# The recurrence of an RWKV-7 layer: another order of work on VectorE and ScalarE, keys scaled earlier, final norms on other banks

## The chip, the cores and the metric

The kernel runs on one core of a Trainium2 chip. The metric is the device time of one execution in microseconds, as the median of several runs. The engines are PE (matrix products; PEld is its loading of weights), DVE (VectorE), ACT (ScalarE), POOL (GpSimd) and SP (SyncE, which issues all the DMAs named here).

## The reference, cut to what matters

A trunk of two layers on 1024 prompt rows with 16 meta rows ahead of them, and on 64 sample rows (8 sequences of 8), 1104 columns in all. Layer 0 is a gated DeltaNet and isn't touched. Layer 1 is RWKV-7 time mixing with 16 heads of 64:

```python
kk = l2norm((k * k_k).reshape(B, T, H, N))
k = k * (1.0 + (a - 1.0) * k_a)
decay = jnp.exp(-jnp.exp(w))
...
def step(S, inp):
    r_t, k_t, v_t, d_t, kk_t, b_t = inp
    S = (S * d_t[:, :, None, :]
         + jnp.einsum('bhvk,bhk->bhv', S, -kk_t)[..., None] * b_t[:, :, None, :]
         + v_t[..., None] * k_t[:, :, None, :])
    return S, jnp.einsum('bhvk,bhk->bhv', S, r_t)
...
y = (y - mean) * lax.rsqrt(var + GN_EPS) * lnx_w.reshape(H, N) + lnx_b.reshape(H, N)
y = y + jnp.sum(r_h * k_h * r_k, -1, keepdims=True) * v_h
y = y.reshape(B, T, D) * jax.nn.silu(z)
return y @ w_o, S, xn[:, -1]
```

After the layer come a residual add and one final RMSNorm (`finish` in the kernel).

## The kernel before

Layer 1 computes the recurrence in chunks of 64 rows. The 1104 columns are three segments (384, 384, 336), the 16 heads eight pairs, so there are 24 **items** n = 8 s + p, each with six chunks. Within a chunk the decays are cumulated: `cs` is their running sum, Dp = exp(-c cs) scales what reads the state, iD = exp(c cs) what writes it. A chunk's inner triangular system is inverted beforehand.

**Projections** (`projections`): PE runs the dense tiles of r, v and z; beside them `system_steps` makes for each item the scaled keys kk (stored as `kpd`), the reads al (`ald`), the plain keys k2 (`k2d`) and the triangular system, `system_inverse` inverts it on GpSimd, `system_merge` finishes it (`ttd`). VectorE also makes the low halves of the weights here.

**The wave** (`wave`): 52 steps tau. In step tau up to three items are in work, item n with its chunk ci = tau - 2n. A step has the phases 0, 1, 1.5, 2 and 3, and the order of all instructions is that in which Python emits them, engine by engine; nothing is reordered. `step_solve` multiplies state and reads (matmuls into `xX` and `rA`, then ACT scales X, L115); `step_inner` applies the inverse (matmuls, then ACT writes UV); `step_values` starts the next step's values; `step_state` adds UV into the state's bank `rA` and into the output, in the same bank, DVE writes the state S (L1921), then ACT copies y (L1922). `step_old` (`pre` on ACT) follows after phase 2.

Around this, `rwkv_item` puts the work of an item into (step, phase, priority), with T = 2n its first step; within a phase the lower priority goes first. Ahead of T: `load` (DMAs, T-4), `exps` (Dp and iD on ACT, T-3), `reads` and `writes` (products on DVE into AR and BK, T-3), `pair` (product of r, r_k and k2, DVE, T-3), `halves` (its split for PE, ACT and POOL, T-2), `scores` (24 matmuls `fG`, then masks on DVE, T-2 and T-1), `values` (transposes of v, ACT copies them into UV, T-2), `bonus` (two matmuls, then `rbv` on DVE, T-2), `keys` (transposes of BK, T-1). Behind it: `stats` for each chunk (DVE), then `rwkv_finish` in five parts: the variance and the power on POOL (L160); the end of the reciprocal root on DVE and the normalised y on POOL (L1945; for n above 21 on ACT with a bias `gnb`); transposes of y and `t` (L1953); `lz` (L1955); the split into yh (ACT) and yl (POOL).

`fill` works off two further lists in shares of a step: the output products `project_out` (three matmuls for each of 4 item tiles, weights by `Stream.take`, which casts a tile with whi on ACT and wlo on POOL and fetches another, then an addition L2042 on DVE), and `finish` for the first two segments: four transposes `dfin` into a bank, a square on ACT (its sum is wanted), a product with the weight on DVE (L2078), twice; then a root, and a scaling on POOL (L2093) and the output DMA.

PSUM has eight banks: tag "r" 3, "f" 2, "x", "z" and "d" 1 each. A tag's next user waits until the last reader of the bank is done.

Of the kernel before, what the change touches and what calls it, by code (L numbers as in the profile page):

```python
# [88 lines left out]
class Builder:  # L89
# [1477 lines left out]
    def system_steps(self, Q, B):  # L1567
# [30 lines left out]
        nc.vector.tensor_tensor(a, a, k, op=ALU.mult)  # L1598
        nc.sync.dma_start(self.ald[Q.n], al)
# [93 lines left out]
    def rwkv_item(self, n, put):  # L1693
# [13 lines left out]
        def load(*names):  # L1707
            src = dict(cs=(self.csd[p], 1), r=(self.rd[p], 2), v=(self.vd[p], 2))
            for x in names:
                if x == "al":  # L1710
                    P.AR = t(self.fp, [128, 6, 2, 64], "AR", 5)
                    nc.sync.dma_start(P.AR[:, :, 0, :], c6(self.ald[n]))
                elif x == "kp":
                    P.BK = t(self.fp, [128, 6, 2, 64], "BK", 2)
                    nc.sync.dma_start(P.BK[:, :, 1 - P.x, :], c6(self.kpd[n]))
                elif x == "tt":
                    P.TT = self.TTz[n % len(self.TTz)]
                    for h in (0, 1):
                        q = slice(64 * h, 64 * h + 64)
                        nc.sync.dma_start(P.TT[q, h].rearrange("p c k -> p (c k)"), self.ttd[n][q])  # L1720
                elif x == "k2":
                    ld[x] = t(self.fp, [128, 384], "fldk2", 2)
                    nc.sync.dma_start(ld[x], self.k2d[n])
                else:
                    d, b = src[x]
                    ld[x] = t(self.fp, [128, 384], "fld" + x, b)
                    nc.sync.dma_start(ld[x], d[:, c0:c0 + 384])

        def exps():
            P.Dp, P.iD = t(self.fp, [128, 384], "fDp", 1), t(self.fp, [128, 384], "fiD", 1)  # L1730
            self.act(P.Dp, ld["cs"], AF.Exp, scale=-self.DEC)
            self.act(P.iD, ld["cs"], AF.Exp, scale=self.DEC)
# [8 lines left out]
        def writes():  # L1741
            nc.vector.tensor_tensor(P.BK[:, :, P.x, :], c6(ld["k2"]), c6(P.iD), op=ALU.mult)

        def pair():
            P.pr = t(self.fp, [128, 384], "pr", 1)
            nc.vector.scalar_tensor_tensor(P.pr, ld["r"], pc("rwkv_r_k"), ld["k2"], op0=ALU.mult, op1=ALU.mult)
# [55 lines left out]
        put(T - 3, 1, exps, 2)  # L1802
        put(T - 3, 2, reads, 2)
        put(T - 3, 3, writes, 1.5)
        put(T - 1 - (n < 3), 2 + (n < 3), lambda: load("tt"), 0)
        put(T - 3, 3, pair, 6)
        put(T - 2, 1, halves, 1)
        put(T - 2, 1, lambda: scores(0), 2)
        put(T - 2, 2, values, 3)
        put(T - 2, 3, bonus, 3)  # L1810
# [3 lines left out]
        if s == 0:  # L1814
# [3 lines left out]
            put(T - 2, 2, go, 5)  # L1818
# [15 lines left out]
        for ci in range(6):  # L1834
            put(T + ci + 1, 1 if ci < 5 else 0, lambda ci=ci: stats(ci), 2.5 if ci < 5 else 0)
        if n < 22:
            f = self.rwkv_finish(P, 0, 6)
            at = [(T + 6, 0, 2), (T + 6, 2, 1.8), (T + 8, 0, 3), (T + 8, 1, 2.2), (T + 8, 2, 0)]
            plans = [(f, at + [(T + 8, 3, 5)] * (s == 2))]
        elif n == 22:  # L1840
            plans = [(self.rwkv_finish(P, 0, 6), [(T + 6, 0, 2), (T + 6, 1, 2), (T + 7, 0, 2.9), (T + 7, 0, 2.95), (T + 7, 1, 2.3),
                                                     (T + 7, 3, 5)])]
        else:
            plans = [(self.rwkv_finish(P, 0, 4), [(T + 4, 1, 3), (T + 4, 3, 2), (T + 5, 0, 3), (T + 5, 0, 3.1), (T + 5, 1, 2)]),
# [63 lines left out]
    def step_state(self, P, ci):  # L1908
# [7 lines left out]
        for h in (0, 1):  # L1916
            self.mmx(P.pY[hs[1 - h]], G[:, ci, h, 64:128], UV[:, ci, h, :], self.first(P, hs[1 - h]))
        if c == 1:
# [3 lines left out]
        nc.scalar.copy(P.y[:, ci], P.pY)  # L1922

    def rwkv_finish(self, P, a, b):
# [6 lines left out]
        zg = t(ap, [128, 384], "lz", 2)  # L1931
# [37 lines left out]
    def rwkv_sample_read(self, P):  # L1969
# [9 lines left out]
        sp = self.ps("f", 2, "sn")  # L1979
# [80 lines left out]
    def finish(self, s, x2):  # L2060
# [3 lines left out]
        for q in range(3):  # L2064
            tt = 3 * s + q
            nr = 80 if tt == 8 else 128
            tags = [(R, R), (R, ("x", 1)), (("d", 1), R)][q] if s == 2 else [("d", 1)] * 2
# [464 lines left out]
    def wave(self, zin, stay, last, pool):  # L2532
# [4 lines left out]
        Z, DD = ("z", 1), ("d", 1)  # L2537
# [16 lines left out]
        jobs += [(lambda s=s, a=a: out(s, a, a + 4, Z, DD), 16, 15 + 16 * s + 2 * a, 23 + 16 * s + 2 * a) for s in (0, 1) for a in (0, 4)]  # L2554
        jobs += [(lambda: out(2, 0, 4, Z, ZF), 16, 47, 51), (lambda: out(2, 4, 6, Z, ZF), 8, 51, 52)]

        more = [(lambda: self.finish(0, X2[0]), 12, 31, 38), (lambda: self.finish(1, X2[1]), 12, 47, 51.5)]
# [102 lines left out]
```

## Time and profile before

| | us |
|---|---|
| median of 3 runs | 2259.64 |
| lowest, highest | 2253.32, 2263.17 |
| profiled execution, its own time | 2267.2 |
| its span (first to last instruction) | 2265.5 |
| start of the first X of the wave in the span | 1791.77 |
| granted clock of TensorE, mean over the span | 0.966 |

Over the span PE is busy for 93%, DVE for 63%, ACT and POOL for 56% each. A line such as "L1921 DVE ... | 31.6, 278 | 14.5 <-PE rA L133 9.6" says: line of the kernel, engine, operation, tiles and shapes, count; busy us in all and mean ns of one; idle us of the engine ahead of them, and what ended it. Matmuls are pipelined, so that a PE that counts as busy need not be at its peak.

### The profile page before, as it was taken

How to read it: one execution, taken by the hardware profiler on the slowest of the kernel's cores; microseconds unless marked ns; L12 is line 12 of the kernel's file. 1: busy time of each engine (PE TensorE's matmuls, PEld its weight loads, DVE VectorE, ACT ScalarE, POOL GpSimd, SP SyncE). 2: the span in 40 equal slices, each digit the busy share in tenths (PEclk: the TensorE clock that was granted, in tenths of full speed). 3: DMA queues.
4: the chain of work that ended last, by engine and by line, in shares of the span. 5: the costliest groups of instructions: out<-in, count | busy, mean ns of one | idle time of the engine just before them, and what ended most of it. 6: DMA issues, size and time to landing. Idle time of an engine off the chain costs nothing. (4 is left out here: it accounts for less than half of the span.)

```text
span 2265.5 us, 56426 instructions
## 1 busy us (share of the span) xinstructions
PE 2108.8 (93%) x20958; PEld 1963.8 (87%) x20958; DVE 1431.0 (63%) x3638; ACT 1268.3 (56%) x3651; POOL 1259.1 (56%) x1902
## 2 busy tenths in 40 slices
PE   7999999999999999989999999999999888988866
PEld 6888989898989999878999999998899777877765
DVE  7858585757576675955345834667654377766634
ACT  6536565655656665555332755647555466766732
POOL 3428586786858585425222622277668446656652
PEclk9989999999999999999999999999999999999977
DMA  4324242424242434346252154777966666554421
GB/s 118 88 62 122 72 133 66 123 77 116 77 113 74 118 85 114 94 115 185 74 157 72 44 181 163 238 227 209 241 185 165 184 152 170 158 165 125 138 90 61
DMA packets 495404, 291.68 MB, mean 129 GB/s; under 512 B 222345, under 2 KB 480506, under 8 KB 495130
## 3 DMA queue, kind: packets, MB, share of 16 engines
q1 hardware_dynamic: 495130, 288.08, 45.2%
q8 instruction: 166, 2.72, 0.5%
q14 instruction: 108, 0.88, 0.1%
HBM read 195.66 MB, written 92.30 MB: 127 GB/s over the span
## 5 line engine op out<-in xcount | busy, mean ns | idle before, releaser
L143 POOL TENSOR_TENSOR wlo<-wraw,whi 128x512 fp32r<-128x512 f32 x190 | 250.6, 1321 | 249.7 <-ACT whi L139 204.6
L692 POOL TENSOR_TENSOR invT<-invT,invtmp 72x31 f32<-72x31 f32 (+36 forms) x341 | 214.5, 629 | 26.7
L634 DVE SCALAR_TENSOR_TENSOR cvy<-raw,cw,cvy 128x408 f32<-128x408 f32 (+2 forms) x288 | 200.9, 697 | 31.1 <-ACT cvy L115 27.1
L690 POOL TENSOR_TENSOR invtmp<-invA,invT 72x31 f32<-72x31 f32 (+36 forms) x341 | 201.3, 590 | 23.4 <-DMA invA<-rltd 3.7
L129 PE MATMUL d<-xc,whi 128*128 128x384 f32 (+1 forms) x640 | 177.3, 342 | 0.0
L139 ACT CAST whi<-wraw 128x512 fp32r<-128x512 f32 x238 | 146.4, 617 | 23.9 <-DMA wraw<-in_rwkv_w_rkvz 9.1
L129 PE MATMUL dv<-xc,whi 128*128 128x384 f32 (+1 forms) x480 | 154.2, 342 | 0.0
L129 PE MATMUL dz<-xc,whi 128*128 128x384 f32 (+1 forms) x480 | 153.6, 343 | 0.0
L115 ACT ACTIVATE w<-rA,nbp 128x128 f32<-128x128 f32 x144 | 45.2, 364 | 151.0 <-PE rA L129 136.3
L129 PEld LDWEIGHTS d<-xc,whi 128*128 128x128 f32 x640 | 118.3, 192 | 1.9 <-ACT ev L1434 0.2
L129 PE MATMUL d<-xc,wlo 128*128 128x384 f32 (+1 forms) x320 | 105.3, 339 | 1.9 <-DVE wlo L143 1.9
L129 PE MATMUL dz<-xa,whi 128*128 128x384 f32 (+1 forms) x288 | 103.1, 358 | 0.5 <-DVE zg L906 0.5
L160 POOL TENSOR_TENSOR ors<-ovar,cvals 128x6 f32<-128x6 f32 x24 | 34.2, 1423 | 124.3 <-DVE ovar L1122 124.3
L129 PE MATMUL dv<-xa,whi 128*128 128x384 f32 (+1 forms) x288 | 102.0, 354 | 0.0
L129 PE MATMUL d<-xa,whi 128*128 128x384 f32 (+1 forms) x336 | 95.9, 338 | 0.2 <-POOL xa L143 0.2
L959 POOL TENSOR_SCALAR Sb<-Sb,eglb 128x128 f32<-128x128 f32 x128 | 89.4, 711 | 5.4 <-DVE usc L752 2.2
L129 PEld LDWEIGHTS dv<-xc,whi 128*128 128x128 f32 x480 | 89.0, 188 | 3.5 <-issue 3.0
L129 PEld LDWEIGHTS dz<-xc,whi 128*128 128x128 f32 x480 | 90.8, 192 | 0.7 <-issue 0.2
L129 PE MATMUL d<-xl,whi 128*128 128x384 f32 (+1 forms) x256 | 82.3, 335 | 0.0
L129 PE MATMUL d<-xh,whi 128*128 128x384 f32 (+1 forms) x256 | 82.2, 333 | 0.0
L129 PE MATMUL d<-xh,wlo 128*128 128x384 f32 (+1 forms) x256 | 82.0, 334 | 0.0
L1945 POOL TENSOR_SCALAR y<-y,mv,grs 128x64 f32<-128x64 f32 x132 | 79.5, 620 | 0.9 <-DVE grs L164 0.9
(560 smaller groups left out, 7369.4 us busy)
## 6 DMA issues: line engine op xcount, KB each, us to landing
wraw<-in_gdn_w_in SPq DMA_DIRECT2D x96, 256.0 KB
wraw<-in_rwkv_w_rkvz SPq DMA_DIRECT2D x74, 256.0 KB
Sb<-in_state_gdn SPq DMA_DIRECT2D x64, 256.0 KB
wraw<-in_rwkv_w_o SPq DMA_DIRECT2D x48, 256.0 KB
E<-drow SPq DMA_DIRECT2D x24, 384.0 KB
attn<-drow SPq DMA_DIRECT2D x24, 384.0 KB
wraw<-in_gdn_w_out SPq DMA_DIRECT2D x36, 256.0 KB
out_s_gdn<-Sb SPq DMA_DIRECT2D x32, 256.0 KB
```

Of the source, the lines that this page charges most:

```text
L115: return self.nc.scalar.activation(out, in_, func, bias=bias, scale=scale, **kw)
L129: self.nc.tensor.matmul(out, lhsT, rhs, start=start, stop=stop)
L139: nc.scalar.copy(hi, x)
L143: e.tensor_tensor(lo, x, hi.bitcast(F32), op=ALU.subtract)
L160: self.nc.gpsimd.tensor_tensor(y, x, half.broadcast_to(sh), op=ALU.pow)
L634: nc.vector.scalar_tensor_tensor(ys[s][:, 0:wd(s)], raws[s][:, k:k + wd(s)], cw[k], ys[s][:, 0:wd(s)], op0=ALU.mult, op1=ALU.add)
L690: v.tensor_tensor(tmp, A[:, j, j + 1:32].unsqueeze(2).broadcast_to([nb, n, m]), Tv[:, j, 0:m].unsqueeze(1).broadcast_to([nb, n, m]), op=AL ...
L692: v.tensor_tensor(Tv[:, j + 1:32, 0:m], Tv[:, j + 1:32, 0:m], tmp, op=ALU.subtract)
L959: nc.gpsimd.tensor_scalar(Sb[g][:, u], Sb[g][:, u], self.eglb[:, hv, 4 * g + u:4 * g + u + 1], None, op0=ALU.mult)
L1945: nc.gpsimd.tensor_scalar(y[:, q], y[:, q], mv[:, q, 0:1], P.rs[:, q:q + 1], op0=ALU.subtract, op1=ALU.mult)
```

## The change

Parts of an item's work are put elsewhere, and some operations go from the wave to the projections:

- `system_steps` multiplies the plain keys by iD before it stores them. `load` brings them straight into their half of BK; `writes`, the exponential iD and the buffer `fldk2` are gone. `pair` uses the scaled reads and the scaled keys, whose decays cancel.
- `step_state` copies y before it writes S.
- `stats` stands in the chunk's own step, phase 2. `rwkv_finish` starts in T+5, its second part is first in phase 2 of T+6, `lz` and the split are in phases 2 and 3 of T+8, behind the fill. For items 22 and 23 the plan is written anew.
- `exps` is in T-4, phase 3; `halves` in T-3 behind `pair`; `bonus` ahead of `values` in phase 2 of T-2.
- the read of a sample's state is a phase earlier, its transposes on bank "d" in place of "f".
- `project_out` uses bank "z" alone for the first two segments. `finish(0)` is spread from step 31 to 45 (to 38 before), and for the second segment the second half of each tile uses "f".

```diff
@@ system_steps @@
         nc.vector.tensor_tensor(a, a, k, op=ALU.mult)
+        nc.vector.tensor_tensor(a, a, iD, op=ALU.mult)
@@ rwkv_item: load, exps, writes, pair @@
                 elif x == "kp":
-                    P.BK = t(self.fp, [128, 6, 2, 64], "BK", 2)
                     nc.sync.dma_start(P.BK[:, :, 1 - P.x, :], c6(self.kpd[n]))
...
-                    ld[x] = t(self.fp, [128, 384], "fldk2", 2)
-                    nc.sync.dma_start(ld[x], self.k2d[n])
+                    P.BK = t(self.fp, [128, 6, 2, 64], "BK", 2)
+                    nc.sync.dma_start(P.BK[:, :, P.x, :], c6(self.k2d[n]))
...
-            P.Dp, P.iD = t(self.fp, [128, 384], "fDp", 1), t(self.fp, [128, 384], "fiD", 1)
+            P.Dp = t(self.fp, [128, 384], "fDp", 1)
             self.act(P.Dp, ld["cs"], AF.Exp, scale=-self.DEC)
-            self.act(P.iD, ld["cs"], AF.Exp, scale=self.DEC)
...
-        def writes():
-            nc.vector.tensor_tensor(P.BK[:, :, P.x, :], c6(ld["k2"]), c6(P.iD), op=ALU.mult)
...
-            nc.vector.scalar_tensor_tensor(P.pr, ld["r"], pc("rwkv_r_k"), ld["k2"], op0=ALU.mult, op1=ALU.mult)
+            nc.vector.scalar_tensor_tensor(c6(P.pr), P.AR[:, :, 1, :], pc("rwkv_r_k"), P.BK[:, :, P.x, :], op0=ALU.mult, op1=ALU.mult)
@@ rwkv_item: the plan @@
-        put(T - 3, 1, exps, 2)
-        put(T - 3, 2, reads, 2)
-        put(T - 3, 3, writes, 1.5)
+        put(*((T - 4, 3) if n else (-3, 1)), exps, 6)
+        put(T - 3, 2, reads, 3.5)
...
-        put(T - 2, 1, halves, 1)
+        put(T - 3, 3, halves, 6.1)
...
-        put(T - 2, 3, bonus, 3)
+        put(T - 2, 2, bonus, 2)
...
-            put(T - 2, 2, go, 5)
+            put(*((T - 3, 3) if n else (-2, 2)), go, 5.5)
...
-            put(T + ci + 1, 1 if ci < 5 else 0, lambda ci=ci: stats(ci), 2.5 if ci < 5 else 0)
+            put(T + ci, 2, lambda ci=ci: stats(ci), 1)
...
-            at = [(T + 6, 0, 2), (T + 6, 2, 1.8), (T + 8, 0, 3), (T + 8, 1, 2.2), (T + 8, 2, 0)]
+            at = [(T + 5, 3, 0), (T + 6, 2, 0), (T + 8, 0, 3), (T + 8, 2, 3.4), (T + 8, 3, 2.5)]
...
-            plans = [(self.rwkv_finish(P, 0, 6), [(T + 6, 0, 2), (T + 6, 1, 2), (T + 7, 0, 2.9), (T + 7, 0, 2.95), (T + 7, 1, 2.3),
-                                                     (T + 7, 3, 5)])]
+            plans = [(self.rwkv_finish(P, 0, 6), [(T + 5, 3, 0), (T + 6, 2, 0.5), (T + 7, 0, 2.9), (T + 7, 0, 2.95),
+                                                     (T + 7, 2, 0.5), (T + 7, 3, 5)])]
...
-            plans = [(self.rwkv_finish(P, 0, 4), [(T + 4, 1, 3), (T + 4, 3, 2), (T + 5, 0, 3), (T + 5, 0, 3.1), (T + 5, 1, 2)]),
+            plans = [(self.rwkv_finish(P, 0, 4), [(T + 3, 3, 0.1), (T + 4, 2, 0.6), (T + 5, 0, 3), (T + 5, 0, 3.1), (T + 5, 2, 0.6)]),
@@ step_state @@
+        nc.scalar.copy(P.y[:, ci], P.pY)
         if c == 1:
             nc.vector.tensor_scalar(S, P.pS, DC[:, ci:ci + 1], None, op0=ALU.mult)
         elif c > 0:
             nc.vector.scalar_tensor_tensor(S, P.pS, DC[:, ci:ci + 1], P.pre, op0=ALU.mult, op1=ALU.add)
-        nc.scalar.copy(P.y[:, ci], P.pY)
@@ rwkv_finish @@
-        zg = t(ap, [128, 384], "lz", 2)
+        zg = t(ap, [128, 384], "lz", 3)
@@ rwkv_sample_read @@
-        sp = self.ps("f", 2, "sn")
+        sp = self.ps("d", 1, "sn")
@@ finish @@
-            tags = [(R, R), (R, ("x", 1)), (("d", 1), R)][q] if s == 2 else [("d", 1)] * 2
+            tags = [(R, R), (R, ("x", 1)), (("d", 1), R)][q] if s == 2 else [("d", 1), ("f", 2) if s else ("d", 1)]
@@ wave @@
-        jobs += [(lambda s=s, a=a: out(s, a, a + 4, Z, DD), 16, 15 + 16 * s + 2 * a, 23 + 16 * s + 2 * a) for s in (0, 1) for a in (0, 4)]
+        jobs += [(lambda s=s, a=a: out(s, a, a + 4, Z), 16, 15 + 16 * s + 2 * a, 23 + 16 * s + 2 * a) for s in (0, 1) for a in (0, 4)]
...
-        more = [(lambda: self.finish(0, X2[0]), 12, 31, 38), (lambda: self.finish(1, X2[1]), 12, 47, 51.5)]
+        more = [(lambda: self.finish(0, X2[0]), 12, 31, 45), (lambda: self.finish(1, X2[1]), 12, 47, 51.5)]
```

More of the change, by code (lines that the diff above doesn't have):

```diff
@@ L2536, in wave @@
         nc, t = self.nc, self.t
-        Z, DD = ("z", 1), ("d", 1)
+        Z = ("z", 1)
         X2 = {}
```

## The prediction

> **What bounds the kernel now.** I first cut the part that the change touches, the recurrence of layer 1, into stretches at its 52 steps (a step begins with the first activation X<-xX). The view of busy time by stage, its columns being stretch: length, busy PE, PEld, DVE, ACT, POOL, granted clock, DMA share, GB/s; the rows are steps 2 to 16, 17 to 30, 31 to 36, 37 to 46, 47 to 49, 50, and 51 to the end:
>
> ```profile
> 1803.14:1919.50 116.36, 101.26 (x1896) 85.10 (x1896) 88.09 (x253) 76.09 (x249) 66.09 (x83) 0.96 0.64 167
> 1919.50:2022.46 102.96, 93.59 (x1785) 83.87 (x1783) 75.58 (x239) 72.48 (x240) 64.33 (x80) 1.00 0.55 156
> 2022.46:2084.13 61.67, 47.47 (x777) 41.90 (x773) 35.77 (x117) 34.53 (x114) 37.31 (x45) 0.86 0.48 139
> 2084.13:2156.87 72.74, 65.99 (x1223) 58.75 (x1214) 49.42 (x176) 50.04 (x171) 49.65 (x61) 0.98 0.44 127
> 2156.87:2194.20 37.33, 26.85 (x281) 24.57 (x281) 14.27 (x41) 12.86 (x43) 19.98 (x23) 0.77 0.35 108
> 2194.20:2218.54 24.34, 11.00 (x97) 10.15 (x97) 7.66 (x28) 7.29 (x23) 9.82 (x9) 0.72 0.19 58
> 2218.54:2265.50 46.96, 31.66 (x192) 29.77 (x190) 20.53 (x54) 10.67 (x28) 14.62 (x14) 0.68 0.20 66
> ```
>
> PE is the busiest engine everywhere, nearly full in the second row, and far from full in the third, fifth and sixth, where it waits and its clock is granted in part only. So time can come back only where PE waits. Single steps show how (steps 9, 16, 22, 23, 31, 39):
>
> ```profile
> 1853.47:1864.01 10.54, 8.33 (x175) 7.96 (x178) 7.64 (x21) 5.67 (x19) 5.68 (x10) 0.84 0.50 134
> 1908.49:1919.50 11.01, 8.55 (x120) 7.07 (x112) 7.63 (x22) 5.24 (x18) 7.87 (x10) 0.85 0.63 164
> 1956.26:1963.78 7.52, 6.67 (x138) 5.94 (x130) 5.95 (x20) 5.03 (x17) 4.38 (x5) 1.00 0.76 216
> 1963.78:1970.70 6.92, 6.56 (x131) 5.92 (x127) 5.00 (x15) 5.09 (x17) 5.32 (x8) 1.00 0.25 74
> 2022.46:2037.49 15.03, 8.98 (x135) 7.90 (x131) 7.34 (x21) 6.42 (x21) 6.66 (x9) 0.78 0.66 193
> 2098.58:2107.47 8.89, 8.04 (x145) 7.41 (x149) 5.31 (x17) 5.20 (x17) 6.02 (x9) 0.81 0.57 162
> ```
>
> A plain pair of steps (22 and 23) takes 14.44 us; steps 9, 16, 31 and 39 are long, and each has a lowered clock. The view of waits over the recurrence names the causes (total us, times, longest us):
>
> ```profile
> ACT y L1922 <- DVE rS L1921: 61.1, 57, 4.2
> ...
> PE dfin L126 <- DVE f2k L2078: 16.8, 5, 4.1
> ACT y L115 <- DVE gnb L1940: 16.0, 3, 6.1
> ...
> ACT f2k L115 <- DMA out_y_prompt<-f2k: 14.4, 3, 6.2
> ...
> PEld fG L129 <- DVE rbv L1757: 10.5, 12, 2.1
> ...
> PEld fG L129 <- ACT UV L1792: 8.3, 8, 1.2
> ...
> PEld do L129 <- DVE Sb L2007: 3.3, 1, 3.3
> ```
>
> The largest is ScalarE's, not PE's, and costs nothing by itself. What it delays is seen on the timeline of step 22, first of three engines and then of ScalarE alone to the end of the step:
>
> ```profile
> 1957.37 0.87 ACT L115 ACTIVATE UV<-rA 64x128 f32<-64x128 f32 x3
> ...
> 1958.29 1.45 DVE L1955 SCALAR_TENSOR_TENSOR lz<-t,lnb,lz 128x384 f32<-128x384 f32 x1
> ...
> 1959.82 0.49 PE L126 MATMUL fVT<-ident,fldv 128*128 128x128 f32 x3
> ```
> ```profile
> 1960.64 0.60 ACT L1922 COPY y<-rA 128x64 f32<-128x64 f32 x3 [2.41 <-DVE rS L1921]
> 1961.13 0.52 ACT L139 CAST yh<-lz 128x384 fp32r<-128x384 f32 x1
> 1961.55 0.62 ACT L139 CAST whi<-wraw 128x512 fp32r<-128x512 f32 x1
> 1962.07 0.96 ACT L1792 COPY UV<-fVT 64x384 f32<-64x384 f32 x2
> 1962.93 0.83 ACT L115 ACTIVATE pre<-rS,DC 128x64 f32<-128x64 f32 x3
> 1963.78 0.31 ACT L115 ACTIVATE X<-xX,rk 128x64 f32<-128x64 f32 x1
> ```
>
> lz stands ahead of the state S on VectorE, y waits 2.41 us for S, and the copies of the transposed values, which free a bank of tag "f" for the score matmuls fG, come last. From y on ScalarE is never idle until X, 3.14 us later: it, not PE, sets when step 23 begins.
>
> **The change part by part.** Prices from the groups:
>
> ```profile
> L139 ACT CAST prh<-pr 128x384 fp32r<-128x384 f32 x24 | 12.5, 519 | 0.2 <-DVE pr L1746 0.2
> L115 ACT ACTIVATE fDp<-fldcs 128x384 f32<-128x384 f32 x23 | 12.2, 530 | 0.0
> L115 ACT ACTIVATE fiD<-fldcs 128x384 f32<-128x384 f32 x23 | 12.1, 528 | 0.0
> ...
> L1742 DVE TENSOR_TENSOR BK<-fldk,fiD 128x384 f32<-128x384 f32 x24 | 13.2, 552 | 0.0
> ...
> L1983 ACT COPY Sb<-fsn 128x512 f32<-128x512 f32 x8 | 4.7, 588 | 0.4 <-PE fsn L126 0.2
> ...
> L1598 DVE TENSOR_TENSOR slda<-slda,sldk 128x384 f32<-128x384 f32 x24 | 18.5, 769 | 0.0
> ...
> L2078 DVE TENSOR_TENSOR f2k<-dfin,fw 128x512 f32<-128x512 f32 x12 | 8.3, 690 | 14.3 <-ACT f2k L115 14.3
> ```
>
> *Keys with inverse decay.* Each of 24 items loses one exponential on ScalarE (0.528) and one product on VectorE (0.552), some 13 us of each engine, none of it on PE's path; 24 products of the form of L1598 (0.769, 18.5 us in all) go to the projections, where PE runs dense tiles over them. I take +1 us there, with bounds 0 and 5: a cast or a system's matmul may come a little later. k2 now lands in BK in six runs of 64 floats a partition instead of one of 384, as the kpd load beside it does. SyncE issues it one phase earlier than BK was claimed before, so it waits for the last key transposes of two items ago; behind it in that queue stand al, v and kp, needed a step later. Zero, because the buffer is free when step T-4 starts.
>
> *y ahead of S, VectorE's rest behind S (steady steps).* y waits for PE alone; S now waits for y. In step 22 y could run from about 1958.3, where UV ends, and S end near 1959.4, before lz. But the end of an even step gets new ScalarE work: yh now stands behind lz and the second fill, and the exponential fDp comes ahead of the next X. From the end of PE's value transposes (1960.3 in the row of fVT, and about 0.5 us later with the bonus matmuls ahead of them; I reckon with 1960.9 for their landing) ScalarE has 0.96 + 0.83 + 0.52 + 0.53 = 2.84 us up to X. That puts X at 1960.9 + 2.84 = 1963.74, against 1963.78 now: the 0.85 us that PE lost at fG comes back as a wait for X. In the other step of a pair the exponentials leave the place between X and UV (about -0.2), and prh (0.519) enters ahead of X behind the product pr (about +0.3). So the 13 plain pairs of steps 17 to 46 give nothing: I take +2 us. Bounds: the whole wait for UV<-fVT gone, -8.3, and +0.8 a pair, +10.
>
> *Bonus ahead of the fill (odd steps 3 to 15, and 39).* There fG waits for rbv, 10.5 us, up to 2.1 at a time. rbv will be done half a step before. I take 7 of the 10.5, the rest turning into waits for X. Steps 9, 16, 39 (and 15, alike) also lost clock: 10.54 x 0.16, 11.01 x 0.15 and 8.89 x 0.19 are about 1.7 us each, 6.7 for the four, of which I take 5. The waits before these dips are no longer than 3.3 us in any row above. The Trainium skill ("TensorE: Matmul & The Clock Gate", Part 1) has the clock halve after an idle window of about 3.4 us; step 9, with shorter waits and a granted clock of 0.84, does not agree. By that rule the 5 us would stay lost and the sum be 22 instead of 27.
>
> *Output tiles on bank "z" alone.* The 3.3 us that "do" waited for Sb in step 16 goes; each "z" tile has half a step to be added. I take -3.
>
> *Sample read a phase earlier on "d".* The next user of "d", the transposes of y, now waits for the 0.588 us copy Sb in the three steps where both occur: +2; the copy ahead of X in the others, 0.4 x 6: +2.5. Both bounded by 0 and double.
>
> *First final norm, two groups of four transposes per two steps less crowded.* Steps 31 to 36 take 61.67, six plain ones 3 x 14.44 = 43.3: 18.4 too much. Afterwards each of six groups costs PE 0.6 to 1.2 (8.98 busy in step 31 with two of them, 6.56 in step 23 with none, at different clocks; I take 0.6); three end an odd step, and the y transposes need their bank, held by a square on ScalarE of L1983's size (0.588) and by L2078 (0.690), behind prh (0.519): 2.2 each with the handing over; three delay X by about 0.8. Together 12.6, so some -5. Bounds 0 and -13.
>
> *The end.* Step 50, on three engines:
>
> ```profile
> 2202.90 0.48 PE L133 MATMUL rA<-UV,BT 128*64 128x64 f32 x4 [7.77 <-ACT UV L115]
> ```
> ```profile
> 2200.59 2.10 ACT L115 ACTIVATE y<-y,gnb,grs 128x64 f32<-128x64 f32 x6 [6.08 <-DVE gnb L1940]
> ```
> ```profile
> 2195.32 3.11 POOL L2093 TENSOR_SCALAR f2k<-f2k,frs 128x512 f32<-128x512 f32 x2 [0.68 <-DVE frs L164]
> 2198.41 1.35 POOL L160 TENSOR_TENSOR grs<-va,cvals 128x6 f32<-128x6 f32 x1
> ```
>
> The power of item 22 waits on GpSimd behind the scaling f2k, gnb and the normalisation y behind it, and UV, which PE needs, behind that. The change starts the power in step 49 ahead of the scaling and puts y after UV: 7.5 us of the 7.77 go. With the second half of each norm tile on "f", PE no longer waits for dfin in step 50 (longest row above: 4.1), nor ScalarE for the second gnb: some 4.5 more. In step 47 the same gives 2, in step 51 the cast yh behind UV 1. In step 48 ScalarE waits 6.2 us for an output DMA and X stands behind it: nothing. Together -15; bounds -5 (one cause gone, the scaling still late) and -22.
>
> **Sum:** 1 + 2 - 7 - 5 - 3 + 4.5 - 5 - 15 = -27.5 against the profiled execution, 2267.2 us (span 2265.5). That run lies 0.3% above the median shown, 2259.64; I take the same 27 us from the median: **2233 us**.
>
> S behind y is priced at zero, since the fill covers S until the next step; without cover (step 50 and 51) it is 0.3 each. The Trainium skill ("PSUM — Partial Sum Buffer", on bank collisions) counts two reads of one bank by two engines as a collision, so one has to wait: the row of 61.1 us agrees, and by it the swap only turns the wait round, with the same sum.
>
> **Rivals.**
> 1. *The clock comes back at the end.* From step 47 on PE is busy 26.85 + 11.00 + 31.66 = 69.5 us at clocks of 0.77, 0.72, 0.68. If with the waits of step 47 and 50 the dips go too and it runs at 0.95 or so, 69.5 x (1 - 0.72/0.95) = 17 us more: about 2215. For: every long wait above has its dip. Against: the tail after 2239 keeps its waits.
> 2. *The waits only change their name.* In step 50 ScalarE now has ten normalisations ahead of the weight casts, and GpSimd the powers ahead of the scaling, whose DMA frees f2k; the early gains turn into waits for X. Then some 6 us are left: 2254. For: step 48 is such a chain already.
> 3. *Slower: ScalarE ahead of X.* yh waits for lz, now VectorE's last work before the fill's addition, and prh for pr. If lz takes 1.45 us as in the row above while GpSimd normalises y, and pr comes 0.5 us late, X is late by 0.9 + 0.8 in each of 23 pairs: 39 us, so 2259.6 - 27 + 39 = 2272. It decides from 1.2 us a pair on. For: VectorE is busy 5.95 of 7.52 us in step 22. Against: it loses the 0.552 product.
>
> **Chances.** The forecast (2220 to 2247) 0.55; the first rival 0.14; the second 0.2; the third 0.08; beyond, 0.03. Range for 8 in 10: 2209 to 2257; the forecast's own is 2220 to 2247. A measurement tells about 0.5% from no change, 11 us. Faster: the forecast, the first rival and a part of the second, 0.77; within 0.5%: 0.15; slower: 0.08.
>
> **What would show it.** Right: no wait of y for rS and none of fG for rbv; steps 22 and 23 together still 14 to 14.8 us, with PE now waiting for X; step 50 under 14 us; steps 31 to 36 some 56. Wrong: plain pairs under 13.8 us (then I overrated ScalarE's queue, and it is faster) or over 15.5 (the third rival); step 50 still over 20 us, with PE waiting for UV or X; long waits for wlo<-wraw,whi in the projections.

## The result and the profile after

The changed kernel takes 2237.87 us (median of 4 runs, 2230.09 to 2244.11) against 2261.4 us for the kernel before (4 runs, 2253.32 to 2266.53): a ratio of 0.9897, 95% interval 0.9851 to 0.9944. The forecast was 2233, faster. The profiled execution of after took 2241.65 us, its span 2239.9, so that the spans differ by 25.6 us where the sum said 27.5.

The total agrees better than its parts. The view of busy time by stage, columns as in the prediction: first steps 2 to 16, 17 to 30, 31 to 36, 37 to 46, 47 to 49, 50, 51 to the end of the kernel after, then its steps 9, 16, 22, 23, 31, 39:

```profile
1825.60:1934.80 109.20, 95.97 (x1890) 81.04 (x1890) 77.30 (x249) 73.95 (x240) 68.75 (x82) 1.00 0.68 171
1934.80:2029.60 94.80, 89.38 (x1761) 81.76 (x1761) 71.07 (x232) 70.74 (x233) 65.94 (x84) 1.00 0.64 173
2029.60:2079.30 49.70, 41.40 (x769) 37.96 (x769) 32.19 (x107) 32.73 (x109) 32.98 (x41) 0.97 0.62 169
2079.30:2150.90 71.60, 64.66 (x1214) 58.91 (x1214) 51.52 (x173) 49.78 (x170) 51.26 (x62) 0.98 0.46 131
2150.90:2182.90 32.00, 22.86 (x281) 21.07 (x281) 15.16 (x46) 12.87 (x44) 21.32 (x23) 0.89 0.41 123
2182.90:2196.20 13.30, 8.62 (x97) 7.84 (x97) 6.49 (x24) 7.28 (x22) 8.95 (x9) 0.86 0.33 112
2196.20:2239.90 43.70, 29.33 (x194) 27.12 (x190) 19.81 (x52) 10.56 (x28) 14.57 (x14) 0.73 0.21 71
...
1875.20:1884.10 8.90, 6.42 (x142) 5.90 (x144) 4.76 (x16) 5.77 (x20) 6.78 (x8) 1.00 0.60 148
1927.00:1934.80 7.80, 7.36 (x138) 5.86 (x130) 6.50 (x21) 5.25 (x18) 5.28 (x8) 1.00 0.75 177
1968.80:1975.70 6.90, 6.53 (x134) 5.75 (x126) 5.28 (x19) 5.16 (x19) 4.38 (x7) 1.00 0.83 212
1975.70:1982.20 6.50, 6.15 (x125) 5.84 (x129) 4.90 (x16) 4.78 (x16) 5.09 (x6) 1.00 0.35 106
2029.60:2040.20 10.60, 7.06 (x124) 6.67 (x128) 5.75 (x17) 5.49 (x19) 6.15 (x7) 0.94 0.74 210
2092.70:2099.20 6.50, 6.13 (x125) 5.81 (x129) 4.93 (x19) 4.77 (x16) 5.66 (x7) 1.00 0.34 103
```

Laid beside the rows of before and the terms of the prediction (its regained clock, 5 us over four steps, is split evenly: 3.8 in steps 9, 15 and 16, 1.2 in 39), in us of the profiled executions. The stretch of the projections runs from the last matmul of the second low-rank factor (tile flora) to the first X of the wave; what is ahead of it is computed by the same instructions in both kernels.

| stretch | before | after | change | predicted |
|---|---|---|---|---|
| up to the last flora matmul | 1414.6 | 1421.1 | +6.5 | 0 |
| projections | 377.2 | 391.7 | +14.5 | +1 |
| steps 0 to 16 | 127.8 | 122.0 | -5.8 | -9.3 |
| steps 17 to 46 | 237.4 | 216.1 | -21.3 | -4.2 |
| steps 47 to the end | 108.6 | 89.0 | -19.6 | -15 |

Two terms are far off with opposite signs. The steady steps gained: steps 22 and 23 together take 13.42 us, not 14.44, and full clock stands in every row from step 9 to 23. The projections lost. The view of waits from 8 us ahead of the first X to the end (total us, times, longest us), PE first and then ScalarE:

```profile
PE rA L133 <- ACT X L115: 21.9, 24, 7.2
PE dyT L129 <- DVE f2k L2073: 11.4, 5, 3.1
PE dsn L126 <- DMA sn<-in_state_rwkv: 8.1, 4, 4.9
PE fG L129 <- DVE rbv L1753: 4.3, 6, 1.6
...
PE dyT L129 <- ACT Sb L1978: 2.3, 3, 0.8
```
```profile
ACT y L115 <- DVE gnb L1935: 6.7, 3, 4.5
...
ACT y L1913 <- PE rA L133: 4.8, 11, 0.8
```

ScalarE's wait of y for the state, 61.1 us before, is gone; y waits for PE alone. PE now waits for X, as the prediction had it. The longest of these waits, 7.2 us, opens step 49, where X stands behind an output DMA; in steps 17 to 46 none is over 1.0 us. New near the top is `dsn`, the transposes of a sample's state, which wait for the DMA that brings it: 4.9 us once ahead of the first X, 3.2 us in steps 2 to 16. ScalarE in step 22 of after, from X to the next X (start, us, operation, idle before):

```profile
1968.78 0.72 ACT L115 ACTIVATE X<-xX,rk 128x64 f32<-128x64 f32 x3
1969.80 0.86 ACT L115 ACTIVATE UV<-rA 64x128 f32<-64x128 f32 x3 [0.30 <-PE rA L133]
1970.62 0.81 ACT L1913 COPY y<-rA 128x64 f32<-128x64 f32 x3
1971.33 0.62 ACT L139 CAST whi<-wraw 128x512 fp32r<-128x512 f32 x1
1973.13 0.96 ACT L1788 COPY UV<-fVT 64x384 f32<-64x384 f32 x2 [1.19 <-PE fVT L126]
1974.00 0.83 ACT L115 ACTIVATE pre<-rS,DC 128x64 f32<-128x64 f32 x3
1974.73 0.50 ACT L139 CAST yh<-lz 128x384 fp32r<-128x384 f32 x1
1975.13 0.52 ACT L115 ACTIVATE fDp<-fldcs 128x384 f32<-128x384 f32 x1
1975.68 0.73 ACT L115 ACTIVATE X<-xX,rk 128x64 f32<-128x64 f32 x3
```

The order is the foreseen one: the copies of the transposed values, `pre`, yh, the exponential, X. The step is 4.35 us up to those copies (1973.13 - 1968.78) and 2.55 us from them to X. In before it was 5.81 and 1.71. Most of what follows can be told in these two numbers.

### The profile page after: what moved, and what is told of

Read it like the earlier page. It is cut to its first block, busy times and chain, and to the rows that moved or that the text cites. A ratio compares the mean times of both kernels' runs of the same rounds, so it can differ in the third digit from the quotient of the medians.

```text
span 2239.9 us, 56232 instructions
## 1 busy us (share of the span) xinstructions
PE 2093.9 (93%) x20958; PEld 1955.0 (87%) x20958; DVE 1430.2 (64%) x3638; ACT 1261.5 (56%) x3627; POOL 1261.8 (56%) x1902
## 5 line engine op out<-in xcount | busy, mean ns | idle before, releaser
L115 ACT ACTIVATE w<-rA,nbp 128x128 f32<-128x128 f32 x144 | 45.3, 364 | 152.8 <-PE rA L129 137.7
```

The source lines that it names most:

```text
L115: return self.nc.scalar.activation(out, in_, func, bias=bias, scale=scale, **kw)
```

## The experiments

The runs e1 to e4, e5 to e8 and e9 to e12 each shared a chip and the runs of the kernel before on it. A ratio with an interval is against those; where none is given, the kernel ran once, and only its trace is read.

**e1_before_again.** The kernel before, unchanged, to see what its trace shows a second time.

> The kernel before, unchanged, profiled a second time: a control for how far stages repeat. In the two profiles so far layer 0 ends 7 us apart (last matmul of the second low-rank factor at 1414.6 and 1421.1 us), though its instructions are the same; from there to the last matmul of the system merges it is 362.1 us before and 371.0 after, from there to the first X 15.0 and 20.7, and the wave 473.7 and 427.2. Theory (the change costs time in the projections): this run repeats 362 (within 2) and 15.0 (within 1). Rival (noise): it comes out anywhere between 362 and 371.

One execution: 2258.95 us. The stretch from flora to the last merge matmul (mU) took 361.4 us (362.1 the first time; after: 371.0), and from there to the first X 15.2 (15.0; after: 20.7). The wave took 469.0 (473.7). But flora ended at 1411.6 instead of 1414.6, and over all runs of this study it ended between 1405.8 and 1421.1, with the same instructions ahead of it: the +6.5 in the table's first row is no effect of the change, while +14.5 in the second is mostly one. The wave of the kernel before varies too: of the 4.7 us between its two profiles, 3.0 lie in steps 47 to the end (108.6 and 105.6) and 1.8 in steps 17 to 46 (237.4 and 235.6). Against this second profile the table's last two changes are -19.5 and -16.6.

**e2_keys_in_wave.** The change, but the keys multiplied in the wave as before.

```diff
-        nc.vector.tensor_tensor(a, a, iD, op=ALU.mult)
...
+            self.act(P.iD, ld["cs"], AF.Exp, scale=self.DEC)
...
+        def writes():
+            nc.vector.tensor_tensor(P.BK[:, :, P.x, :], c6(ld["k2"]), c6(P.iD), op=ALU.mult)
...
+        put(T - 3, 3, writes, 1.5)
```

> The changed kernel with one part undone: the product with the inverse decay goes back into the wave (exponential iD, product into BK, the load into a buffer of its own; that buffer is single here). Theory A (the product in the projections delays the systems): projections (last low-rank matmul to last merge) back from 371 to about 362, and the wave longer by 0.5 us a pair through the exponential ahead of X, about +10 us, so the total within 3 us of the changed kernel. Rival B (the projections only vary): projections stay near 371, the total 10 us slower than the changed kernel. Rival C (the iD work was hidden): wave unchanged at 427, total 9 us faster.

Ratio 0.9932 (0.99 to 0.9963). Flora to mU fell to 363.3 us, but the wave rose from 427.2 to 446.4: this part of the change pays about 19 us in the wave of these two profiles, where I had written nothing. Not all of it need be the two operations: 7.9 us lie in steps 2 to 16, where PE was busy for 102.83 us in place of 95.97 at a granted clock of 0.93 in place of 1.00, and the five executions of this kernel range from 2235.28 us (mean clock 0.977) to 2251.75 (0.968), with the profiled one at 2249.64. Steps 17 to 46 give 11.2 us, which agrees with the single pair: steps 22 and 23 take 14.21 us. (The buffer of the plain keys is single here; SyncE's load waits for it 0.6 us at most, and no engine waits for what it loads.) ScalarE there, the step's two X and what stands ahead of the second, then the end of step 23:

```profile
1966.70 0.72 ACT L115 ACTIVATE X<-xX,rk 128x64 f32<-128x64 f32 x3
...
1970.97 0.96 ACT L1792 COPY UV<-fVT 64x384 f32<-64x384 f32 x2 [1.17 <-PE fVT L126]
...
1973.38 0.51 ACT L115 ACTIVATE fiD<-fldcs 128x384 f32<-128x384 f32 x1
1973.92 0.72 ACT L115 ACTIVATE X<-xX,rk 128x64 f32<-128x64 f32 x3
...
1980.49 0.51 ACT L139 CAST prh<-pr 128x384 fp32r<-128x384 f32 x1 [0.78 <-DVE pr L1746]
```

In the even step the exponential of iD stands between the copies and X (2.95 us in place of 2.55). In the odd step the product into BK stands ahead of `pr` on VectorE, and prh, which X stands behind, waits 0.78 us for it; in after that wait is 0.31. Both operations were on the path, through ScalarE's queue.

**e3_sn_late.** The transposes of item 1's sample state a phase later, for the dsn wait ahead of the wave (the edit names item 0 too, but its transposes stand at that place already).

```diff
-            put(*((T - 3, 3) if n else (-2, 2)), go, 5.5)
+            put(*((T - 3, 3) if n > 1 else (T - 2, 2)), go, 5.5)
```

> The changed kernel with the transposes of the sample states of items 0 and 1 back in phase 2 of T-2, on bank d as in the change. Theory: the 4.9 us that PE waits just before the first X (for the state's DMA) go, the way from the last merge to the first X falls from 20.7 to about 16, the total by about 4. Rival: the wait moves to another DMA or to bank d and the total stays.

Ratio 0.985 (0.9832 to 0.9869). From mU to the first X it took 14.9 us, as in before, 5.8 us less than in after. But the wave took 431.3 us, 4.1 more: 1.6 of it in steps 0 and 1, where a part of the wait now is,

```profile
PE dsn L126 <- DMA sn<-in_state_rwkv: 2.6, 1, 2.6
```

and 2.4 in steps 2 to 16, which took between 107.6 and 111.4 us in the kernels that differ from after elsewhere only (e4, e8, e10). So the wait is for one DMA's data, not for the bank; moving its reader removed it ahead of the wave, and of the 5.8 us a net 1.7 shows in these two profiles (447.9 and 446.2 us from mU to the end).

**e4_y_behind_S.** The copy of y behind the state again, all else as in after.

```diff
-        nc.scalar.copy(P.y[:, ci], P.pY)
         if c == 1:
...
+        nc.scalar.copy(P.y[:, ci], P.pY)
```

> The changed kernel with y copied after S again, all else as changed. Theory A (what gains in the plain steps is the order on VectorE, since lz and the statistics no longer stand ahead of S): plain pairs stay near 13.4 us, up by at most 0.2, total +0 to +3. Rival B (the order of y and S gains): pairs back to 14 us or more, wave +8 or more.

Ratio 0.9878 (0.9859 to 0.9896), indistinguishable from after. A pair of steps took 13.64 us instead of 13.42: the even step 6.83 for 6.90, the odd one 6.80 for 6.52. In step 22 the wait that the change's name speaks of came back as

```profile
1962.01 0.75 ACT L1917 COPY y<-rA 128x64 f32<-128x64 f32 x3 [0.41 <-DVE rS L1916]
```

which is 0.41 us, not the 2.41 of before. Once VectorE's other work is behind the state, which of y and S goes first matters little: 0.2 us a pair. What the swap alone is worth in the order of before was not run.

**e5_keys_alone.** The kernel before with the part on the keys alone.

```diff
+        nc.vector.tensor_tensor(a, a, iD, op=ALU.mult)
...
-            self.act(P.iD, ld["cs"], AF.Exp, scale=self.DEC)
...
-            nc.vector.tensor_tensor(P.BK[:, :, P.x, :], c6(ld["k2"]), c6(P.iD), op=ALU.mult)
...
+            nc.vector.scalar_tensor_tensor(c6(P.pr), P.AR[:, :, 1, :], pc("rwkv_r_k"), P.BK[:, :, P.x, :], op0=ALU.mult, op1=ALU.mult)
```

> The kernel before with the key part of the change alone (product with the inverse decay in the systems, k2 loaded into BK, no iD in the wave, the pair product from scaled reads and keys); every place in the plan as before. In the changed kernel, undoing this part made a plain pair 0.8 us longer (14.21 against 13.42) and the wave 19 us, and took the projections from 371 to 363 us. Theory A (it is worth that because the changed plan puts the exponentials ahead of X; in the old plan iD lay between X and UV): here a plain pair falls by 0.2 to 0.3 only (14.44 to about 14.2), the wave by some 5, the projections grow by 4 to 9, the total is within 5 us of before. Rival B (the key part carries the gain by itself): pairs at 13.7 or less, wave down by 15 or more, total down by 8 or more.

Ratio 0.9965 (0.9947 to 0.9983; 10 runs, 17 of before). The wave took 460.5 us (before 473.7 and 469.0), flora to mU 366.6 (362.1 and 361.4). The pair went from 14.44 to 13.54. So what moved is nearly the whole gain of the steady steps, and it needs no other part of the change. Busy time by stage, steps 22 and 23:

```profile
1949.56:1956.60 7.04, 6.66 (x138) 5.93 (x130) 5.55 (x17) 5.02 (x18) 4.37 (x5) 1.00 0.85 231
1956.60:1963.10 6.50, 6.32 (x131) 5.82 (x127) 5.04 (x16) 4.62 (x17) 5.26 (x8) 1.00 0.22 68
```

Why the even step lost 0.48 us is on VectorE's timeline of the kernel before, and on ScalarE's of this one:

```profile
1955.28 0.55 DVE L1742 TENSOR_TENSOR BK<-fldk,fiD 128x384 f32<-128x384 f32 x1
...
1960.34 0.65 DVE L1921 SCALAR_TENSOR_TENSOR rS<-rA,DC,pre 128x64 f32<-128x64 f32 x3
```
```profile
1953.46 0.60 ACT L1917 COPY y<-rA 128x64 f32<-128x64 f32 x3 [1.93 <-DVE rS L1916]
...
1954.89 0.96 ACT L1788 COPY UV<-fVT 64x384 f32<-64x384 f32 x2
```

In before, the product into BK starts 0.98 us ahead of the step's X, in a queue of VectorE that hardly pauses up to the state S, five microseconds later. Everything behind it, S included, comes half a microsecond later for it; y waits for S (2.41 us in before, 1.93 here), and the copies of the values stand behind y (5.81 us after X in before, 5.33 here).

**e9_keys_with_exp.** The same, but the exponential of iD is still computed on ScalarE and read by nothing; the product alone is gone from VectorE.

```diff
+            iD = t(self.fp, [128, 384], "fiD", 1)
+            self.act(iD, ld["cs"], AF.Exp, scale=self.DEC)
```

> The key part alone on the kernel before, with the exponential iD still computed on ScalarE at its old place into a buffer that nobody reads; so of the wave only the product into BK on VectorE is gone. The key part alone took a plain pair from 14.44 to 13.54. Theory A (VectorE: without the 0.55 us product ahead of pr, the statistics and lz, the state of the next even step is ready earlier and with it y and the copies of the transposed values): pairs stay below 13.8. Rival B (ScalarE: the exponential between X and UV): pairs back to 14.2 or more.

One execution, 2256.49 us; the pair took 13.95 us, between the theories:

```profile
1954.14:1961.17 7.03, 6.66 (x138) 5.94 (x130) 5.54 (x17) 5.02 (x17) 4.35 (x5) 1.00 0.79 222
1961.17:1968.09 6.92, 6.56 (x131) 5.92 (x127) 4.96 (x16) 5.08 (x18) 5.31 (x8) 1.00 0.26 79
```

The two rows settle it. The even step is that of e5 (7.03 and 7.04), the odd step is that of before (6.92); the other pairs of steps 18 to 29 agree within 0.02 us. VectorE's product was worth 0.49 us in the even step, ScalarE's exponential 0.42 in the odd one, where it stood between X and UV. Each operation costs most of its own duration (0.552 and 0.528), each in another step.

**e6_norms_old.** The change with the statistics and the plan of the group norm of items 0 to 21 at their old places.

```diff
+            if n < 22:
+                put(T + ci + 1, 1 if ci < 5 else 0, lambda ci=ci: stats(ci), 2.5 if ci < 5 else 0)
...
-            at = [(T + 5, 3, 0), (T + 6, 2, 0), (T + 8, 0, 3), (T + 8, 2, 3.4), (T + 8, 3, 2.5)]
+            at = [(T + 6, 0, 2), (T + 6, 2, 1.8), (T + 8, 0, 3), (T + 8, 1, 2.2), (T + 8, 2, 0)]
```

> The changed kernel with the statistics and the parts of the group norm back at their old places for items 0 to 21 (lz and statistics ahead of the state on VectorE, yh and yl in phase 2), y still ahead of S. Theory A (VectorE's order ahead of S is what made plain pairs long): S is late by lz and the statistics again, pairs 13.9 or more, wave +8 or more against 427. Rival B (with y ahead of S a late S is covered by the fill): pairs within 0.2 of 13.4, wave within 4.

Ratio 0.9863 (0.9829 to 0.9897): not to be told from after. Neither expectation came. The pair is shorter, 13.07 us against 13.42, since yh now stands ahead of the copies of the values, where ScalarE had time, and not between them and X:

```profile
1960.43 0.51 ACT L139 CAST yh<-lz 128x384 fp32r<-128x384 f32 x1 [0.84 <-PE zo L129]
...
1961.37 0.96 ACT L1788 COPY UV<-fVT 64x384 f32<-64x384 f32 x2
```

The copies start 4.38 us after this step's X (1956.99), and X follows them by 2.13 us (1963.50): 6.51 for the step. Against that, steps 31 to 46 rose from 121.3 to 126.3 us and steps 47 to 50 from 45.3 to 48.9. "Other work behind the state" costs the plain steps 0.35 us a pair and pays where norms of two kinds and the end meet.

**e7_fold_sn.** The change with one VectorE product less in the projections (k is multiplied by iD once, and both keys are made from it), and the late sample reads of e3.

```diff
-        nc.vector.scalar_tensor_tensor(kk, k, pc("rwkv_k_k"), a, op0=ALU.mult, op1=ALU.mult)
...
-        nc.vector.tensor_tensor(kk, kk, iD, op=ALU.mult)
+        nc.vector.tensor_tensor(iD, k, iD, op=ALU.mult)
+        nc.vector.scalar_tensor_tensor(kk, iD, pc("rwkv_k_k"), a, op0=ALU.mult, op1=ALU.mult)
...
-        nc.vector.tensor_tensor(a, a, k, op=ALU.mult)
         nc.vector.tensor_tensor(a, a, iD, op=ALU.mult)
```

> The changed kernel with two repairs: the plain keys are first multiplied by the inverse decay, into the buffer of the sum, and both kk and the stored keys are made from that, so that no product is added (four operations on VectorE instead of five for each item); and the sample states of items 0 and 1 transposed in phase 2 of T-2. Theory: projections back to 362 to 364 (from 371), the way from the last merge to the first X 15 (from 20.7), wave 427 to 431 as in the run with the late transposes, total about 2223, that is 0.982 to 0.985 of before. Rival (the projections' extra time is not the added product but the later store of the keys or the six runs of each load): projections stay at 366 to 371 and the total at the 2228 of the late transposes alone.

Ratio 0.9832 (0.9805 to 0.9859). Flora to mU took 363.0 us, and 14.7 from there to X. Over the study that stretch took 361.4, 362.1 and 363.3 without the product, 364.4 to 371.0 with it (nine profiles, median 366.6), 363.0 and 364.9 with it folded in. The product costs 4 to 5 us of that stretch. The waits that grow are not always the same ones. The view of waits over the projections of before and of after has

```profile
PE mZ L129 <- DMA sTT<-r_u: 3.6, 4, 1.6
```
```profile
PE mZ L129 <- DMA sTT<-r_u: 8.0, 5, 4.3
```

but with the same products in e3 this wait was 3.9 us, in e5 7.9: it varies with the execution, so that no single wait can be named as the place of the loss.

**e8_tail_plan_old.** The plan of items 22 and 23 as it was.

```diff
-            plans = [(self.rwkv_finish(P, 0, 6), [(T + 5, 3, 0), (T + 6, 2, 0.5), (T + 7, 0, 2.9), (T + 7, 0, 2.95),
-                                                     (T + 7, 2, 0.5), (T + 7, 3, 5)])]
+            plans = [(self.rwkv_finish(P, 0, 6), [(T + 6, 0, 2), (T + 6, 1, 2), (T + 7, 0, 2.9), (T + 7, 0, 2.95),
+                                                     (T + 7, 1, 2.3), (T + 7, 3, 5)])]
...
-            plans = [(self.rwkv_finish(P, 0, 4), [(T + 3, 3, 0.1), (T + 4, 2, 0.6), (T + 5, 0, 3), (T + 5, 0, 3.1), (T + 5, 2, 0.6)]),
+            plans = [(self.rwkv_finish(P, 0, 4), [(T + 4, 1, 3), (T + 4, 3, 2), (T + 5, 0, 3), (T + 5, 0, 3.1), (T + 5, 1, 2)]),
```

> The changed kernel with the plan of items 22 and 23 as before (power in phase 0 of T+6, root and normalisation in phase 1 ahead of UV). Theory: in step 50 PE waits 7 us or more for UV again; steps 50 to the end grow from 57.0 to 66 or more. Rival (the gain of the end comes from the second half of each norm tile on bank f): step 50 grows by 3 or less.

One execution, 2233.29 us. Step 50 took 21.8 us instead of 13.3, and its one long wait is the old one:

```profile
PE rA L133 <- ACT UV L115: 7.8, 1, 7.8
```

**e10_finish_old.** The first two segments' final norm on bank "d" alone, and the first one's work in steps 31 to 38 again.

```diff
-            tags = [(R, R), (R, ("x", 1)), (("d", 1), R)][q] if s == 2 else [("d", 1), ("f", 2) if s else ("d", 1)]
+            tags = [(R, R), (R, ("x", 1)), (("d", 1), R)][q] if s == 2 else [("d", 1)] * 2
...
-        more = [(lambda: self.finish(0, X2[0]), 12, 31, 45), (lambda: self.finish(1, X2[1]), 12, 47, 51.5)]
+        more = [(lambda: self.finish(0, X2[0]), 12, 31, 38), (lambda: self.finish(1, X2[1]), 12, 47, 51.5)]
```

> The changed kernel with the final norms as before: finish of the first segment spread over steps 31 to 38, both halves of each tile on bank d. Theory (the forecast's price): steps 31 to 46 take 5 us more than the 121 of the changed kernel, steps 47 to 50 take 4 to 6 more than 45 to 47. Rival A (most of the 12 us that steps 31 to 36 lost come from here): steps 31 to 46 take 10 or more longer. Rival B (they come from the plain pairs): 2 or less.

One execution, 2240.10 us. Steps 31 to 46 and 47 to 50, by stage:

```profile
2013.22:2143.45 130.23, 109.77 (x1983) 99.69 (x1983) 84.24 (x280) 82.49 (x275) 83.86 (x102) 0.93 0.49 136
2143.45:2195.44 51.99, 34.17 (x378) 30.93 (x378) 21.81 (x70) 20.28 (x66) 30.52 (x31) 0.81 0.33 105
```

Over both stretches the wait of the final norm's transposes for their bank is back:

```profile
PE dfin L126 <- DVE f2k L2073: 18.1, 5, 4.8
```

Against after that is +8.9 us in the first stretch (spreading the first norm) and +6.7 in the second (bank "f"; 2.7 of it in step 50).

**e11_bonus_old.** The bonus behind the values again, in phase 3 of the same step.

```diff
-        put(T - 2, 2, bonus, 2)
+        put(T - 2, 3, bonus, 3)
```

> The changed kernel with the bonus behind the values and the fill again (phase 3 of T-2). Theory (the forecast's price): PE waits for rbv before the score matmuls of odd steps again, steps 2 to 16 take 7 to 12 us more than 109 to 112, step 15 and 9 with a lowered clock; plain pairs about as changed. Rival (with the keys out of the wave VectorE is early enough anyway): steps 2 to 16 within 3 us, plain pairs within 0.2 of 13.4.

One execution, 2236.91 us. Steps 2 to 16 by stage, and PE's longest wait in them:

```profile
1812.95:1934.42 121.47, 104.74 (x1882) 88.28 (x1880) 78.30 (x248) 74.23 (x240) 67.89 (x81) 0.92 0.60 153
```
```profile
PE fG L129 <- DVE rbv L1753: 10.7, 8, 2.1
```

The same view of before, over its steps 2 to 16, has

```profile
PE fG L129 <- DVE rbv L1757: 6.4, 6, 1.8
```

Steps 2 to 16 take 12.3 us more than in after (7 for the bonus and 3.8 of the clock were forecast there): PE is busy for 8.8 us longer (104.74 and 95.97, at a clock of 0.92 and 1.00) and idle for 3.5 us longer. They also take 5.1 us more than in before. But the plain pair took 13.07 us, 0.35 less, which I had not foreseen: without the bonus ahead of them the values' transposes come earlier. ScalarE's copies of them start 4.00 us after X (1967.70), not 4.35:

```profile
1971.70 0.96 ACT L1788 COPY UV<-fVT 64x384 f32<-64x384 f32 x2 [0.82 <-PE fVT L126]
```

**e12_fold_sn_norms.** e7, with the group norm of items 0 to 11 at the old places, where e6 had been shorter, and that of the others at the new.

```diff
+            if n < 12:
+                put(T + ci + 1, 1 if ci < 5 else 0, lambda ci=ci: stats(ci), 2.5 if ci < 5 else 0)
...
+            if n < 12:
+                at = [(T + 6, 0, 2), (T + 6, 2, 1.8), (T + 8, 0, 3), (T + 8, 1, 2.2), (T + 8, 2, 0)]
```

> The two repairs (keys folded, late sample transposes of items 0 and 1) and the group norm of items 0 to 11 at its old places, since the old places gave plain pairs of 13.07 against 13.42 but longer steps 31 to 50. Theory (yh late in an even step, behind lz and just ahead of X, costs the 0.35 us a pair): steps 17 to 30 take 92 us against 94.7, steps 31 to the end as in the repairs alone, the total 2 to 3 us below their 2223. Rival (the old places cost in the early steps with sample work what they gain later): total within 1 us of the repairs alone.

Ratio 0.9814 (0.9793 to 0.9834): the shortest of all, 2216.54 us (2212.71 to 2223.0). Steps 17 to 30 took 92.0 us (e7: 94.7), the pair 13.08; steps 31 to 36 took 53.5 (e7: 49.7), so that much of it was given back. Its interval overlaps that of e7; that of after, which begins at 0.9851, it does not reach. In the profiles e12 is shorter than after by 6.1 us from flora to mU (364.9 and 371.0) and by 2.8 from there to the end (445.1 and 447.9); the rest lies ahead of the change, where executions differ, so that the share of the edits in this ratio is not settled.

## Why the prediction was right, and where it was not

**Keys with inverse decay: wrong.** The failed step is "none of it on PE's path". The quoted timeline had the end of the path in it: ScalarE sets when the next step begins, its copies of the values stand behind y, and y waits for S. The product into BK stands five microseconds further up VectorE's queue, ahead of the rows quoted. I counted what the two operations take of two engines that are not the bottleneck, and did not ask what is queued behind them. In the order of before they are worth 0.9 us a pair (e5, e9), in the new order 0.8 (e2), by other ways.

**Steady steps: wrong in size, right in mechanism.** "Plain pairs under 13.8 us" was my own sign of being wrong, of having overrated ScalarE's queue, and it came. PE waits for X, ScalarE's queue from the copies to X sets the step, and PE's lost time at fG is gone. But +2 us for steps 17 to 46 was wrong, and the lower bound of -8.3 too near: 13 pairs at 14.44 - 13.42 = 1.02 are 13 us less. Two terms were mis-sized by 0.29 us each. The copies were put at 4.64 us after X (1960.9 - 1956.26) and came at 4.35: the bonus matmuls delay the copies by 0.35 us (4.00 in e11), where I had reckoned 0.6 from 1960.3 to 1960.9. And the four operations up to X were summed by their durations, 2.84 us, where the starts in the row of step 22 above span 2.55: each of the first three is followed by an operation that starts 0.09 to 0.10 us before it ends. The Trainium skill ("ScalarE: Activation LUTs", What ACT_TABLE_LOAD costs) says that activations back to back overlap by some 93 ns; the trace agrees, and three such overlaps are the whole difference. In the odd step I had the exponential's leaving at 0.2 and prh's coming at 0.3; the first is 0.42 by e9. The second came to next to nothing in sum with all else that moved, since the odd step takes 6.50 us in e5 without it and 6.52 in after.

**y ahead of S: right in the new order, open in the old.** Priced at zero; 0.2 us a pair (e4): once S is early, the wait of y is short in either order. That the 61.1 us of before cost "nothing by itself" is not shown. There the wait stood on the path of e5, ahead of the copies of the values. In e6 the statistics and lz stand ahead of S again and y doesn't wait for it; its even step takes 6.50 us and the copies start 4.38 us after X, where e5, with y behind S, has 7.03 and 5.33. The two kernels differ in other places as well, so no price of the swap alone follows.

**Projections: too low.** +1 with bounds 0 and 5 for the product; about 4.5 by medians of the study, at the upper bound; the 371.0 us of after are the longest of the nine profiles. Not in the sum at all was the wait of dsn ahead of the wave, 4.9 us in the view of waits and 5.8 by e3: I had counted the sample's transposes against the bank that they moved to, and forgot to ask whether their data had landed a phase earlier.

**Bonus and clock in steps 2 to 16: the sum near, the terms not.** 7 and 3.8 us were forecast for these steps, 12.3 measured by e11, but split the other way: 8.8 in PE's busy time at the lower clock and 3.5 in its idle time. And that is what the place is worth in the new order. Against the kernel before these steps gave 7.2 us, of which 5.3 are PE's busy time (101.26 and 95.97, the clock 0.96 and 1.00) and 1.9 its idle time. The step that failed is "I take 7 of the 10.5": the 10.5 us were PEld's over the whole wave, PE itself waited 6.4 us for rbv in steps 2 to 16, and 4.3 are left. The rest of the change had +1.5 in the sum for these steps (4.5 for the samples less 3 for "do"); by e11 against before it costs 5.1, clock included. The 2 us forecast for the transposes of y behind Sb measured 2.3. For the copy ahead of X 2.5 were forecast; what the view has instead is 3.2 us in which dsn waits for its DMA. The wait of "do" for Sb is gone, as foreseen.

**First final norm: right in mechanism, too small.** -5 was said; spreading it is worth 8.9 us over steps 31 to 46 (e10), 3.7 of them in PE's busy time (109.77 and 106.06, the clock 0.93 and 0.97). Steps 31 to 36 took 49.7 us, not 56: six plain steps are 3 us shorter as well, and the wait for f2k that is left in step 31 is 3.1 us.

**The end: right, with some luck in the parts.** Step 50 was forecast 12 us shorter and is 11.0 shorter; e8 puts 8.4 of it on the plan of items 22 and 23 (7.5 forecast), e10 2.7 on bank "f" (4.5 forecast). Steps 47 to 49 and 51 gave 5.3 and 3.3 in place of 2 and 1; of the 3.3, 2.1 lie between the two profiles of before (46.95 and 44.87).

**The rivals.** The first, the clock at the end, came in half: the clock rose from 0.77, 0.72 and 0.68 to 0.89, 0.86 and 0.73, and PE's busy time there fell from 69.5 to 60.8 us, 8.7 of the 19.6 us gained after step 46; its 17 would have needed 0.95. The second did not come: step 48's wait of ScalarE for an output DMA is left (6.5 us, and PE waits 7.2 for the X behind it), but from step 47 on no new long one took the place of those removed. The third did not come either: X stands behind yh and prh, but in steps 22 and 23 yh waits for nothing and prh 0.3 us.

The total was close, then, by luck in good part, because errors cancel: 17.1 us more gain than forecast in steps 17 to 46 and 4.6 more at the end stand against 13.5 more loss in the projections, 3.5 less gain in steps 0 to 16, and 6.5 us ahead of the change, where executions differ.

## What to carry to other kernels

An operation on an engine that is far from full is not free: look at what is queued behind it on that engine and follow that to the bottleneck; half a microsecond taken from VectorE's queue, five microseconds ahead of the state that it delays, gave back half a microsecond in e5 and in e9. Sum a queue by the distance of starts in the trace, not by durations, and give a moved load two prices: that of the bank or buffer it takes, and that of its data arriving when the reader has moved. The longest wait in a view (here 61.1 us) tells no price by itself: with an early releaser the order behind it was worth 0.2 us a pair, so price what makes the releaser late.

## What the runs showed of the hardware

A lowered clock was seen without any long wait of PE. In e11 no wait of PE in steps 2 to 16 was longer than the 2.1 us on rbv, and the granted clock was 0.92 over 121 us. In after it was 1.00 over the same steps, whose longest waits are

```profile
PE fG L129 <- DVE rbv L1753: 4.3, 6, 1.6
PE dsn L126 <- DMA sn<-in_state_rwkv: 3.2, 3, 1.7
```

The Trainium skill ("TensorE: Matmul & The Clock Gate", Part 1) speaks of an idle window of some 3.4 us; these rows show a lowered clock with no wait as long as that. Neither the longest wait nor the sum orders the runs. The length of steps 2 to 16 less PE's busy time is 16.7 us in e11 (clock 0.92), 14.3 in e2 (0.93), 13.2 in after (1.00) and 10.8 in e12 (0.98); PE's longest idle stretch there is 1.6 us in e2 and 1.1 in e12.

The clock records of the traces show what the means hide. They have two values alone, 1.00 and 0.50, and in the wave the clock changes only on a grid of 3.41 us, which lies at another place of the span in each execution. In e11 the clock is 0.50 in four stretches of steps 2 to 16, from 1836.01, 1870.14, 1887.21 and 1904.28, of 6.83, 3.41, 3.41 and 6.83 us; in the 3.41 us ahead of the first, PE was busy for 1.50. After and e4 have no such stretch in these steps, e10 and e3 one, e8 two, though they differ elsewhere, so a few microseconds between two profiles can be the clock's alone. What makes the clock fall was not tried.

The same instructions ahead of the change ended between 1405.8 and 1421.1 us in the runs of this study, a spread of 15 us. Against that, a change of a few microseconds in the wave is read from the stretch between two fixed instructions, not from the total.
